# Sparse attention: tile 1's query rotation in quarters after three ticks, and a later place for tile 1's steps

## The chip, the core and the metric

One core of one Trainium2 chip runs the whole program in one launch. The metric is the device time of one execution in microseconds, the median of the runs. A profiled execution lists every instruction of five engines: TensorE (PE, with its weight loads as PEld), VectorE (DVE), ScalarE (ACT), GpSimd (POOL) and SyncE (SP, which issues the DMAs).

## The reference, cut to what matters

Two transformer blocks of two layers each run over 256 tokens of width 1024. The part that the change touches is the attention of the second block's first layer: 16 query heads in 4 groups, three branches (compressed keys, selected blocks, window), weighted by gates. With 256 tokens there are only four blocks of 64 keys, so every block is selected, and the two wide branches are two causal softmaxes.

```python
proj = x @ w_in
q = rope(proj[..., :ATTN_WIDTH].reshape(B, S, N_HEADS_2, hd))
...
s_c = jnp.einsum('bgrqd,bgcd->bgrqc', qb, k_cmp)
p_c = masked_softmax(s_c, cmp_end[None, :] <= t[:, None])
o_c = jnp.einsum('bgrqc,bgcd->bgrqd', p_c.astype(v_cmp.dtype), v_cmp)
...
return gb[:, 0][..., None] * o_c + gb[:, 1][..., None] * o_s + gb[:, 2][..., None] * o_w
```

`rope` multiplies the two halves of each head of 64 by a cosine and a sine table: y1 = x1 c - x2 s and y2 = x2 c + x1 s.

## The kernel before

The 256 tokens are two tiles of 128 (tile 0 and tile 1). Matrix products run as three passes over a high and a low part of each operand (`mm3`, L270 to L274): the high part is a cast on ACT (L264), the low part a subtraction on DVE, or on POOL where `ASIDE` says so (L265; L267 and L268 where a scale comes with it).

Nothing is scheduled at run time: the order of the instructions on each engine is the order in which the program writes them out. Work that is to lie beside other work is a generator. `tick` (L222) advances every waiting generator by one `yield`, and `turnover` (L252) is a tick and a step of the weight stream (`pump`), which splits the next weight blocks into high and low.

In `nsa` (L1322) the query projection of tile 0 runs ahead and that of tile 1 follows block by block (`late`). After a tile's last block `queries(t)` (L1508) is begun as a generator: it rotates the tile's queries out of PSUM with `rope64` (L1306: six DVE instructions, L1314 to L1320, over a number of heads), in two halves of 8 heads with a `yield` after each, and then transposes them in two groups of four (L352) and splits the transposes into `xa` (L267, L268).

The attention of a tile is `unit(t)`: `attend` (L988) runs 16 steps of two heads' scores in a software pipeline. One step of it issues, in this order: s, the scores of step i (L281 and L272 to L274 on PE, into one of two PSUM banks of that tile); e, the exponentials of step i-1 (L1057 on ACT); m, the maxima of step i (L1050 on DVE); c, the weights of step i-2 (L1612, L1614 on DVE, L1073 on POOL); t, the transposes of step i-4 (L1634 on PE, with the high cast L1066); l, their low parts (L1063 on DVE); p, the product with the values of step i-5 on odd steps. Beside it `compressed(t)` computes the scores against the compressed keys (24 products of 32 columns on PE, tile `kc`) and their softmax on DVE (L1562 to L1577), in pieces between ticks.

`weave` (L1003) lays the two tiles' steps in a row by the string `FILL["nsa"]`: "0" and "1" are a step of that tile followed by a tick, "c" is a late block of a projection (nothing where none is left), "w" a block of the output projection. The first "1" begins tile 1's unit, and its `join` finishes `queries(1)` on the spot, whatever it has still to issue:

```python
            def join(t):
                nonlocal wp
...
                self.finish(qs[t])
```

At the first "w" tile 0's remaining steps are issued, at the string's end those of tile 1.

Of the kernel before, what the change touches and what calls it, by code (L numbers as in the profile page):

```python
# [53 lines left out]
POOLED = {"rope": "vv", "nsa": "gg", "fox": "vv"}  # L54
FILL = {"nin": "qlqlqlqlqlqqllqlkklkkkkklkkkkkkkkkllll",
        "da": "c0c0c0c0c0011011100101101010ww1w111w",
        "nsa": "ccc00c0c10c0010010010010111010101001011101w00w0u10",
        "fox": "0cc0cc0c0c0c0111010101011010011w1w1w1w"}
WARM = {"da": (1, 1), "nsa": (0, 0), "fox": (0, 0)}
ASIDE = {"go": "0234567", "wo": "0234567", "w10": "03", "w11": "", "nwo": "034567", "fwo": "0123457"}  # L60
DONE = object()

# [12 lines left out]
class Stream:  # L75
# [11 lines left out]
    def aside(self, key):  # L87

        name, c = key[:-1], key[-1]
        while isinstance(name, tuple):  # L90
            name = "".join(str(x) for x in name) if not isinstance(name[0], tuple) else name[0]
        return str(c) in ASIDE.get(name, "")

# [110 lines left out]
class Build:  # L204
# [883 lines left out]
    def diff_attention(self, xt, vx):  # L1088
# [3 lines left out]
        with tc.tile_pool(name="da", bufs=1) as gp, tc.tile_pool(name="daw", bufs=2) as wp:  # L1092
# [48 lines left out]
            def unit(t):  # L1141
# [68 lines left out]

                return self.attend(H, ORDER["da"], WARM["da"], s=scores, m=peak, e=soft, c=scale, t=turn, l=low, p=pv)

# [109 lines left out]
    def nsa(self):  # L1322
# [3 lines left out]
        with ExitStack() as ctx:  # L1326
# [12 lines left out]
            wq = ctx.enter_context(tc.tile_pool(name="nar", bufs=2))  # L1339
# [168 lines left out]
            def queries(t):  # L1508
                x = self.scr()
                x3 = x.rearrange("p (h d) -> p h d", d=64)  # L1510
                if POOLED["rope"][t] == "g":
                    y = self.scr()
                    for q in range(2):
                        nc.scalar.copy(y[:, HALVES[q]], self.A[t].halves[q])
                        self.rope64(x3[:, 8 * q:8 * q + 8], y[:, HALVES[q]].rearrange("p (h d) -> p h d", d=64), t, 8,
                                    wq, nc.gpsimd)
                        yield
                else:
                    for q in range(2):
                        self.rope64(x3[:, 8 * q:8 * q + 8], self.A[t].halves[q].rearrange("p (h d) -> p h d", d=64), t,  # L1520
                                    8, wq)
                        yield
                for _ in range(WAITS["q"]):
                    yield
                yield from self.transpose_split(x, qT, 0, 8, slice(t * P, t * P + P), 0.125)

            qs, tails = [], []
            steps = {"q": self.ahead([("n0", c) for c in range(KC)], xt, lambda t: qs.append(self.begin(queries(t)))),
                     "k": compress()}
            for i, x in enumerate(FILL["nin"]):  # L1530
# [52 lines left out]
            def unit(t):  # L1583
# [88 lines left out]

                return self.attend(16, ORDER["nsa"], WARM["nsa"], s=scores, m=peak, e=soft, c=scale, t=turn, l=low, p=pv)

# [8 lines left out]
    def fox(self):  # L1683
# [3 lines left out]
        with ExitStack() as ctx:  # L1687
# [108 lines left out]
            def unit(t):  # L1796
# [61 lines left out]

                return self.attend(8, ORDER["fox"], WARM["fox"], s=scores, m=peak, e=soft, c=scale, t=turn, l=low, p=pv)

# [365 lines left out]
```

## Time and profile before

| what | value |
|---|---|
| time, median of 3 runs | 2741.74 us (2736.85 to 2742.47) |
| profiled execution: its own time | 2738.46 us |
| its span, first to last instruction | 2736.4 us |
| PE busy | 2660.6 us (97%) |
| DVE busy | 2033.9 us (74%) |
| ACT busy | 1337.7 us (49%) |
| POOL busy | 142.6 us (5%) |
| mean granted TensorE clock | 0.981 of full |

The page gives busy times over the whole span; a stage is read from the stretches. The attention that the change touches lies from 806 us to 906 us of the span: it begins with tile 0's first scores and ends where the output projection takes PE over. A row of the timeline reads: start, duration (both us), engine, line, operation, written tile, read tiles, shapes, and in brackets the idle time of the engine before it with what ended it. Two instructions that follow each other on one engine overlap a little in their records, so the price of one in a chain is the distance of the starts. PEclk is the granted clock of TensorE: 1.00 is 2.4 GHz and 0.50 is 1.2 GHz.

### The profile page before, as it was taken

The numbers are of one execution on the slowest core, as the hardware profiler recorded it, in microseconds if no ns is written. First come the engines' busy times: TensorE is split into PE (matmuls) and PEld (weight loads), VectorE is DVE, ScalarE is ACT, GpSimd is POOL, SyncE is SP. The second block draws the span as 40 slices with busy tenths as digits, with TensorE's granted clock in tenths as the row PEclk, the third lists the DMA queues.
The fourth block names the chain that finished last, engine by engine and source line by source line (L and its number), as shares of the span: only waits on it lengthen the run. The fifth ranks groups of instructions, "written<-read, shape, count | busy, mean of one in ns | idle before, by whom it ended". The sixth has DMA issues, their size and how long they took to land.

```text
span 2736.4 us, 44261 instructions
## 1 busy us (share of the span) xinstructions
PE 2660.6 (97%) x17478; PEld 2306.4 (84%) x17478; DVE 2033.9 (74%) x3494; ACT 1337.7 (49%) x2061; POOL 142.6 (5%) x130
## 2 busy tenths in 40 slices
PE   8999999999879999999999999999999999999999
PEld 6789777898757899999977788877999999877887
DVE  6655766655776689988899865555799888899654
ACT  5554654545555544444444454454444444444543
POOL 2200021000123000000000000020000000000000
PEclk9999999999988999999999999998999999999999
DMA  6555552563550336655555575451366555555753
GB/s 234 187 195 177 167 162 76 190 190 128 175 192 1 131 111 192 183 177 168 170 169 170 173 235 187 141 168 46 120 190 185 186 167 172 164 171 171 237 190 107
DMA packets 125235, 448.40 MB, mean 164 GB/s; under 512 B 15058, under 2 KB 15586, under 8 KB 125028
## 3 DMA queue, kind: packets, MB, share of 16 engines
q1 hardware_dynamic: 122404, 437.45, 50.3%
q0 software_dynamic: 2624, 8.14, 1.0%
q8 instruction: 136, 2.23, 0.3%
q14 instruction: 71, 0.58, 0.1%
HBM read 444.49 MB, written 1.05 MB: 163 GB/s over the span
## 4 chain that ended last, share of the span: by engine, by line
PE 60%; DVE 6%; ACT 1%; issue 1%; DMA 0%; ACTq 0%
PE A L536 25%; PE B L272 8%; PE B L274 8%; PE B L273 8%; PE A L464 6%; PE B L2046 2%; DVE lob L265 2%; PE B L352 0%; PE A L436 0%; DVE topi L1903 0%; DVE topi L1906 0%; PE A L272 0%; PE B L1835 0%; DVE top L1905 0%; DVE oh L1948 0%
## 5 line engine op out<-in xcount | busy, mean ns | idle before, releaser
L264 ACT CAST hib<-raw 128x1024 fp32r<-128x1024 f32 x519 | 544.3, 1051 | 735.6 <-PE B L274 349.4
L265 DVE TENSOR_TENSOR lob<-raw,hib 128x1024 fp32r<-128x1024 f32 x508 | 619.5, 1221 | 193.8 <-ACT hib L264 193.6
L272 PE MATMUL B<-xa,hib 128*128 128x256 f32 x2096 | 593.1, 283 | 0.0
L273 PE MATMUL B<-xa,lob 128*128 128x256 f32 x2096 | 587.6, 280 | 0.2
L274 PE MATMUL B<-xa,hib 128*128 128x256 f32 x2096 | 586.7, 280 | 0.0
L536 PE MATMUL A<-hib,xa 128*128 128x512 f32 x1440 | 411.7, 399 | 2.0 <-ACT xa L264 2.0
L273 PEld LDWEIGHTS B<-xa,lob 128*128 128x128 f32 x2096 | 394.6, 188 | 1.5 <-DVE lob L265 1.2
L272 PEld LDWEIGHTS B<-xa,hib 128*128 128x128 f32 x2096 | 394.5, 188 | 0.0
L274 PEld LDWEIGHTS B<-xa,hib 128*128 128x128 f32 x2096 | 394.3, 188 | 0.0
L536 PEld LDWEIGHTS A<-hib,xa 128*128 128x128 f32 x1440 | 265.7, 188 | 62.5 <-ACT xa L264 2.4
L265 DVE TENSOR_TENSOR lox<-raw,hix 128x1024 fp32r<-128x1024 f32 x174 | 212.3, 1232 | 120.6 <-ACT hix L264 120.4
L264 ACT CAST hix<-raw 128x1024 fp32r<-128x1024 f32 x192 | 198.2, 1044 | 137.9 <-PE A L536 85.5
L536 PE MATMUL A<-lob,xa 128*128 128x512 f32 x720 | 226.7, 396 | 0.0
L2053 DVE SCALAR_TENSOR_TENSOR H<-B,H 128x512 f32<-128x512 f32 x128 | 170.3, 1332 | 2.3 <-PE B L2046 1.9
L536 PEld LDWEIGHTS A<-lob,xa 128*128 128x128 f32 x720 | 135.2, 188 | 32.8
L464 PE MATMUL A<-hix,xb 128*128 128x512 f32 (+1 forms) x520 | 157.3, 400 | 3.7 <-ACT gates L1423 2.6
L536 PE MATMUL A<-hix,xa 128*128 128x512 f32 x480 | 133.3, 395 | 0.0
L268 DVE SCALAR_TENSOR_TENSOR lox<-raw,gcol,hix 128x1024 fp32r<-128x1024 f32 (+1 forms) x75 | 92.8, 1250 | 36.2 <-ACT hix L267 36.1
L464 PE MATMUL A<-hix,xa 128*128 128x512 f32 x380 | 114.5, 402 | 3.0 <-ACT hix L267 3.0
L464 PEld LDWEIGHTS A<-hix,xb 128*128 128x128 f32 x520 | 95.8, 193 | 24.2 <-ACT gates L1423 3.9
L536 PEld LDWEIGHTS A<-hix,xa 128*128 128x128 f32 x480 | 90.0, 187 | 22.0
L265 DVE TENSOR_TENSOR xa<-H,xa 128x256 fp32r<-128x256 f32 x256 | 106.2, 419 | 2.9 <-ACT xa L264 2.9
(518 smaller groups left out, 4678.2 us busy)
## 6 DMA issues: line engine op xcount, KB each, us to landing
raw<-in_u SPq DMA_DIRECT2D x256, 512.0 KB, 3.6
raw<-in_v SPq DMA_DIRECT2D x256, 512.0 KB, 3.7
raw<-in_f_w_down SPq DMA_DIRECT2D x64, 512.0 KB, 4.5
raw<-in_w_up SPq DMA_DIRECT2D x48, 512.0 KB, 3.7
raw<-in_l_w_in SPq DMA_DIRECT2D x40, 512.0 KB, 3.9
raw<-in_b_w_qkv SPq DMA_DIRECT2D x24, 512.0 KB, 4.2
raw<-in_a_w_in SPq DMA_DIRECT2D x16, 512.0 KB, 5.2
raw<-in_f_w_up SPq DMA_DIRECT2D x16, 512.0 KB, 3.7
```

Source lines behind the costliest of these rows:

```text
L264: nc.scalar.copy(hi, src)
L265: engine.tensor_tensor(lo, src, hi.bitcast(F32), op=ALU.subtract)
L268: nc.vector.scalar_tensor_tensor(lo, src, scale, hi.bitcast(F32), op0=ALU.mult, op1=ALU.subtract)
L272: mm(out, s[0], m[0], start=start, stop=False, **kw)
L273: mm(out, s[1], m[0], start=False, stop=False, **kw)
L274: mm(out, s[0], m[1], start=False, stop=stop, **kw)
L464: self.nc.tensor.matmul(out[:, 512 * q:512 * q + n], xs[u], w[v][:, n * q:n * q + n], start=start and i == 0, stop=stop and i == 2)
L536: self.nc.tensor.matmul(self.A[t][:, n0:n0 + 512], x[u][:, ts_], w[v][:, n0:n0 + 512], start=first and q == 0, stop=last and q == 2)
L2046: nc.tensor.matmul(p[:, t, :], A[:, t].rearrange("p a b -> p (a b)"), B[q][:, t].rearrange("p a b -> p (a b)"), start=q == 0, stop=q == 1)
L2053: nc.vector.scalar_tensor_tensor(hv, p, 1.0 / G_SCALE, hv, op0=ALU.mult, op1=ALU.mult)
```

## The change

`queries` gets a wait in ticks before the rotation, none for tile 0 and three for tile 1. The rotation is done in four quarters of 4 heads instead of two halves of 8; tile 0 still yields after every second quarter, tile 1 after each. The string puts eight "0" ahead of the first "1" instead of three; from there the two strings run alike but for one "1" fewer ahead of the output projection (15 instead of 16).

```diff
-        "nsa": "ccc00c0c10c0010010010010111010101001011101w00w0u10",
+        "nsa": "ccc00c00c0c0c0010010010010111010101001011101w00w0u10",
...
+ROPE_WAIT = (0, 3)
...
-                    for q in range(2):
-                        self.rope64(x3[:, 8 * q:8 * q + 8], self.A[t].halves[q].rearrange("p (h d) -> p h d", d=64), t,
-                                    8, wq)
+                    for _ in range(ROPE_WAIT[t]):
                         yield
+                    for q in range(4):
+                        self.rope64(x3[:, 4 * q:4 * q + 4], self.A[t].halves[q // 2][:, q % 2 * 256:q % 2 * 256 + 256]
+                                    .rearrange("p (h d) -> p h d", d=64), t, 4, wq)
+                        if t or q % 2:
+                            yield
```

What this does to the order is seen at three places. Line numbers of the changed kernel are higher by 1 up to the rotation and by 4 behind it.

First, DVE around tile 1's rotation (written to `scr` from the banks `A_69` and `A_70`). Before, the halves stand ahead of and behind the value splits `vc`, and the first maxima (L1050) come behind both:

```order
L265 TENSOR_TENSOR kc_5618<-B_71,kc_5617 64x4x16 x2
L1314 TENSOR_TENSOR scr_6429<-A_69,rope_tab_5606 128x8x32
L1315 TENSOR_TENSOR rw_6430<-A_69,rope_tab_5606 128x256
L1316 TENSOR_TENSOR scr_6429<-scr_6429,rw_6430 128x8x32
L1317 TENSOR_TENSOR scr_6429<-A_69,rope_tab_5606 128x8x32
L1319 TENSOR_TENSOR rw_6435<-A_69,rope_tab_5606 128x256
L1320 TENSOR_TENSOR scr_6429<-scr_6429,rw_6435 128x8x32
L265 TENSOR_TENSOR vc_5616<-B_72,vc_5615 16x256 x4
L1314 TENSOR_TENSOR scr_6429<-A_70,rope_tab_5606 128x8x32
```

Now the splits and the first two maxima come first, and the first quarter (L1315 to L1321) stands ahead of the first piece of tile 0's compressed softmax (L1566 on) and of the third maxima:

```order
L266 TENSOR_TENSOR vc_5616<-B_72,vc_5615 16x256 x4
L1051 TENSOR_REDUCE sm_6480<-A_67 128x2
L1051 TENSOR_REDUCE sm_6509<-A_68 128x2
L1315 TENSOR_TENSOR scr_6445<-A_69,rope_tab_5606 128x4x32
L1316 TENSOR_TENSOR rw_6511<-A_69,rope_tab_5606 128x128
L1317 TENSOR_TENSOR scr_6445<-scr_6445,rw_6511 128x4x32
L1318 TENSOR_TENSOR scr_6445<-A_69,rope_tab_5606 128x4x32
L1320 TENSOR_TENSOR rw_6516<-A_69,rope_tab_5606 128x128
L1321 TENSOR_TENSOR scr_6445<-scr_6445,rw_6516 128x4x32
L1566 TENSOR_TENSOR scr_6528<-B_73,cmask 128x256
L1568 TENSOR_REDUCE sm_6531<-scr_6528 128x16
L1569 TENSOR_TENSOR scr_6528<-scr_6528,sm_6531 128x256
```

The other three quarters follow one each behind the third, fourth and fifth maxima; twelve DVE instructions of 256 elements have become 24 of 128, for tile 0 as well, whose quarters stand where its halves stood.

Second, PE at tile 0's first scores (bank `A_67`). Before, the first four transposes of tile 1's rotated queries (L352) stand between the scores of step 0 and the compressed scores (`kc`), and the other four behind step 1:

```order
L272 MATMUL A_67<-nkT_5611,xa_84 128x2x128
L273 MATMUL A_67<-nkT_5611,xa_85 128x2x128
L274 MATMUL A_67<-nkT_5612,xa_84 128x2x128
L352 MATMUL B_71<-ident,scr_6429 128x128 x4
L272 MATMUL B_73<-kc_5617,xa_84 128x32
```

Now they stand behind the transposes of steps 1 and 2, ahead of steps 6 and 7; here the first four:

```order
L274 MATMUL A_68<-nkT_5611,xa_85 128x2x128
L275 MATMUL A_68<-nkT_5612,xa_84 128x2x128
L1638 MATMUL B_72<-ident,e_6539 128x128 x2
L353 MATMUL B_71<-ident,scr_6445 128x128 x4
L282 LDWEIGHTS identb
L282 MATMUL A_67<-maskb,identb 128x2x128
```

Tile 1's first scores and its 24 compressed scores, which stood behind step 2 of tile 0, now stand behind step 7.

Third, PE where two steps of tile 1 follow each other with no product between them (a score group into `A_69`, four transposes, a score group into `A_70`). Before, the program has two such pairs; this is the second:

```order
L272 MATMUL A_70<-nkT_5611,xa_84 128x512
L273 MATMUL A_70<-nkT_5611,xa_85 128x512
L274 MATMUL A_70<-nkT_5612,xa_84 128x512
L1634 MATMUL B_72<-ident,e_7112 128x128 x4
L281 LDWEIGHTS identb
L281 MATMUL A_69<-maskb,identb 128x2x128
L272 MATMUL A_69<-nkT_5611,xa_84 128x512
```

Now there are four, two of them in one run of three steps:

```order
L275 MATMUL A_69<-nkT_5612,xa_84 128x512
L1638 MATMUL B_72<-ident,e_6796 128x128 x4
L282 LDWEIGHTS identb
L282 MATMUL A_70<-maskb,identb 128x2x128
L273 MATMUL A_70<-nkT_5611,xa_84 128x512
L274 MATMUL A_70<-nkT_5611,xa_85 128x512
L275 MATMUL A_70<-nkT_5612,xa_84 128x512
L1638 MATMUL B_71<-ident,e_6850 128x128 x4
L282 LDWEIGHTS identb
L282 MATMUL A_69<-maskb,identb 128x2x128
```

The other two stand further on, close to the end of tile 1's scores. SP's DMAs stand in the same order in both programs.

## Rows read from the trace of the kernel before

**Rows 1.** The page: the granted clock in 40 slices of the span, in tenths.
```profile
PEclk9999999999988999999999999998999999999999
```

**Rows 2.** Stretches: start:end length, busy PE PEld DVE ACT POOL, PEclk, DMA, GB/s.
```profile
806.00:820.00 14.00, 9.95 (x43) 8.69 (x43) 11.58 (x19) 5.42 (x12) 5.58 (x5) 0.50 0.45 161
820.00:838.75 18.75, 17.79 (x64) 13.31 (x64) 10.90 (x38) 6.07 (x29) 3.32 (x6) 0.50 0.00 0
887.00:890.00 3.00, 3.00 (x16) 3.00 (x15) 1.13 (x4) 1.73 (x6) 1.04 (x1) 0.50 0.00 0
```

**Rows 3.** PE's waits, 745 to 905 us: total, times, longest.
```profile
PE B L352 <- DVE scr L1320: 7.9, 3, 3.9
```

**Rows 4.** Timeline: a rotation of keys (4 heads), tile 0's first half, PE behind it.
```profile
744.88 0.28 DVE L1314 TENSOR_TENSOR dup<-k,rope_tab 128x128 f32<-128x128 f32 x1
...
746.34 0.28 DVE L1314 TENSOR_TENSOR dup<-k,rope_tab 128x128 f32<-128x128 f32 x1
...
754.61 0.41 DVE L1314 TENSOR_TENSOR scr<-A,rope_tab 128x256 f32<-128x256 f32 x1
...
756.50 0.43 DVE L1320 TENSOR_TENSOR scr<-scr,rw 128x256 f32<-128x256 f32 x1
...
756.99 1.07 PE L352 MATMUL B<-ident,scr 128*128 128x128 f32 x4 [3.88 <-DVE scr L1320]
```

**Rows 5.** Timeline: tile 1's second half beside POOL's splits, and PE behind it.
```profile
809.08 0.42 DVE L265 TENSOR_TENSOR vc<-B,vc 16x256 fp32r<-16x256 f32 x1 [0.43 <-ACT vc L264]
...
811.05 2.38 POOL L265 TENSOR_TENSOR lox<-raw,hix 128x1024 fp32r<-128x1024 f32 x1 [4.97 <-ACT hix L264]
...
813.96 2.36 POOL L265 TENSOR_TENSOR lox<-raw,hix 128x1024 fp32r<-128x1024 f32 x1
...
814.41 2.20 DVE L1320 TENSOR_TENSOR scr<-scr,rw 128x256 f32<-128x256 f32 x1
...
816.66 1.12 PE L352 MATMUL B<-ident,scr 128*128 128x128 f32 x4 [3.82 <-DVE scr L1320]
```

**Rows 6.** A stretch that holds tile 0's compressed softmax on DVE.
```profile
819.50:823.55 4.05, 4.05 (x14) 2.67 (x13) 3.72 (x14) 1.81 (x9) 0.61 (x1) 0.50 0.02 9
```

**Rows 7.** Timeline: exponentials of one step on ACT, first and last row.
```profile
817.03 0.37 ACT L1057 ACTIVATE e<-A,sm 128x128 f32<-128x128 f32 x1 [4.50 <-issue]
...
817.63 0.20 ACT L1057 ACTIVATION_READ_ACCUMULATOR e<-A,sm 128x1 f32 x1
```

**Rows 8.** Timeline: PE, pieces at the low and at the full clock.
```profile
805.94 0.42 PE L281 MATMUL A<-maskb,identb 128*128 128x256 bf16 x1
...
822.52 0.39 PE L272 MATMUL B<-kc,xa 128*128 128x32 f32 x1
...
825.74 0.40 PE L281 MATMUL A<-maskb,identb 128*128 128x256 bf16 x1
...
827.01 0.39 PE L272 MATMUL B<-kc,xa 128*128 128x32 f32 x1
...
831.86 0.37 PE L281 MATMUL A<-maskb,identb 128*128 128x256 bf16 x1 [0.96 <-ACT e L1057]
...
833.10 0.69 PE L1634 MATMUL B<-ident,e 128*128 128x128 f32 x2
...
837.54 0.56 PE L272 MATMUL B<-pt,nv 128*128 128x256 f32 x1
...
838.97 0.30 PE L281 MATMUL A<-maskb,identb 128*128 128x256 bf16 x1
...
841.13 0.27 PE L281 MATMUL A<-maskb,identb 128*128 128x256 bf16 x1
...
841.88 0.44 PE L1634 MATMUL B<-ident,e 128*128 128x128 f32 x2
```

**Rows 9.** Timeline: PE at the two pairs of tile 1's steps.
```profile
855.87 0.27 PE L281 MATMUL A<-maskb,identb 128*128 128x256 bf16 x1 [1.11 <-ACT e L1057]
...
885.60 0.27 PE L281 MATMUL A<-maskb,identb 128*128 128x256 bf16 x1 [1.16 <-ACT e L1057]
```

## The prediction

> **What bounds the kernel now.** First the granted clock on the page: full in nearly every slice, with its two lowest slices around 800 us [rows 1]. Then the stretches there: from 806 to 838.75 us, the head of the attention that the change reorders, PE runs at half clock; in the first 14 us of it it is busy for 9.95, in the 18.75 behind them for 17.79 [rows 2]. Then who is waited for: of PE's waits between 745 and 905 us the largest in total is for `scr` of L1320, the last instruction of a query rotation, 7.9 us in three waits [rows 3]. The timeline gives two of them: 3.9 us for tile 0's first half at 757 us [rows 4] and 3.8 us for tile 1's second half at 816.7 us [rows 5]; the third is what is left, 0.2. So PE bounds this stage, and it loses time by two waits for a rotation on DVE and by the low clock. The edit to tile 1 aims at the second wait; the first is tile 0's and is only made longer.
>
> **Tile 0's rotation in four pieces.** Six DVE instructions over 8 heads take 2.32 us (from 754.61 to the end of L1320 at 756.93); six over 4 heads take 1.46 (744.88 to 746.34) [rows 4]. A half as two quarters is 2.92, so 0.60 more, twice. PE sits idle ahead of 757 us until the first half is done [rows 4], so the first 0.60 has no cover. The second stands behind it on DVE ahead of the split that PE's next transposes need. I take both, **+1.2 us**; the low end is 0, if the weight loads behind it set the pace until 800 us anyway, and the high end 1.3.
>
> [...]
>
> **Tile 1's rotation moved: the wait that goes.** Gone are the 3.8 us and the 0.2 behind the halves. What is late next has to be followed through DVE, in its new order: value splits, maxima 0 and 1, quarter 1, first piece of the compressed softmax, maxima 2, quarter 2, second piece, maxima 3, quarter 3, maxima 4, quarter 4, maxima 5. PE's order is scores 0, 15 compressed products, scores 1, 9 of them, scores 2, scores 3 and so on; scores 3 use the bank of scores 1 and wait for exponentials 1, and on ACT these stand behind the exponential of the compressed softmax.
>
> PE at half clock: a score group is 1.27 us (825.74 to 827.01), 15 compressed products 3.22 (822.52 to 825.74), so 9 are 1.93 [rows 8]. From 805.94, where the scores of step 0 start [rows 8], scores 2 end at 805.9 + 3 x 1.27 + 5.15 = 814.9. On DVE the four splits `vc` stand 0.85 apart (0.42 of work, 0.43 of wait for ACT); the third started at 809.08 with the first half's last instructions ahead of the first, and without these I take the fourth to end near 809.5 instead of 810.4 [rows 5]; maxima 0 behind them, maxima 1 once scores 1 end (811.7). Quarter 1 starts at 812.1 and comes to its last instruction at 813.4. That one, like L1320 of before, reads two tiles of SBUF, and the rows show what that costs beside POOL: 2.20 us, from 814.41 to 816.61, while POOL's split ran from 813.96 to 816.32; alone it was 0.43 [rows 4, 5]. POOL's two splits come some 0.9 us earlier than before, since ACT casts for them right behind `vc`: the second runs from 813.1 to 815.5. So quarter 1 ends at 815.7.
>
> [...]
>
> From 815.7 the first piece of the softmax takes 1.3 (three instructions [rows 6]), its exponential on ACT 0.4, exponentials 1 0.8 (817.03 to 817.83) [rows 7]: scores 3 start at 818.3. PE idles from 814.9 to 818.3, **3.4 us in place of 4.0**. The wait has changed its name, not gone.
>
> **Then DVE sets the pace.** From 815.7: piece one 1.3; second piece 2.1 (the stretch of 4.05 us holds both pieces, one maxima and two small operations [rows 6]); three quarters 3 x 1.46; four maxima 4 x 0.45; three pairs of small operations and a fourth 4 x 0.35; two low parts 2 x 0.42; the split of PE's new transposes 0.7. Sum 12.5, to 828.2. PE has less than that to do there (scores 3 to 6, four transposes twice) and idles for it in two more pieces. Behind 828.2 follow two transposes, six products, four transposes, scores 7 and two transposes. A pair of transposes is recorded with 0.69, which overlaps the next instruction by some 0.2, so 0.5; the six products are 1.43 (837.54 to 838.97) [rows 8]; four transposes are recorded with 1.12 [rows 5], and I take 0.7. That is 0.5 + 1.43 + 0.7 + 1.27 + 0.5 = 4.4: PE stands at 832.6 with steps 0 to 7 of tile 0 scored. At 839.0 in the trace, where the distances between PE's instructions turn to those of the full clock, steps 0 to 6 were scored and, of tile 1, two steps and the 24 compressed products. What the new program has more to do from there: 24 compressed products, 5.15 at half clock and 3.0 at full by the ratio of the score groups (0.75 to 1.27 [rows 8]); two score groups of tile 1, taken as 1.1 each at full clock (1.5 x 0.75, twice the columns in three of four products); less one score group and two transposes of tile 0, 1.05. That is 4.2, so 836.8 against 839.0: **-2.2 us**, if the clock is full from 832.6 on. Before, it rose at 839.0, 7.1 us after PE's last idle time ended at 831.86 [rows 8]; from 828.2 the same gives 835.4, 2.8 us at half clock, which costs 1.2. **Front of the attention: -1.0.** If the clock rises only behind tile 1's compressed products, near 842.6, the cost is 4.1 and the front ends at +1.9. In the trace it did not rise while PE went through 24 of them from 822.52 on [rows 2, 8], so I give this a large share.
>
> **The later steps.** At both pairs of tile 1's steps with no product between, PE waited 1.1 and 1.2 us for exponentials [rows 9]. The new order has four such pairs: two more, **+2.2**; from 0 (other waits fall in the same place) to 5.3, where each also drops the clock as the second did: 3 us of busy PE at half clock behind it, 1.5 lost [rows 2]. One step of tile 1 more stands behind the two blocks of the output projection; its chain to the transposes has 5 us of PE's products over it, and I take 0. SP's order is unchanged, and no transfer moves.
>
> **Sum.** 1.2 - 1.0 + 2.2 = +2.4 us. Against the profiled execution's own 2738.46 that is 2740.9; that execution lies 3.3 below the median, and the same 2.4 on the median of 2741.74 gives **2744.1**.
>
> **The rivals.**
>
> Slower: the clock. If it stays low until tile 1's compressed products are through (front +1.9) and falls at each added pair (2.2 + 3.0), the sum is 1.2 + 1.9 + 5.2 = +8.3, 2750.0. It decides between 832 and 836 us: a clock that has not risen when those products begin. For it: they are 5 us of narrow products, and they now stand in the dense part. Against it: one of the two pairs of before (855.9) left the clock alone.
>
> Faster: with the long wait cut up, the clock comes back during steps 3 to 7 and not at 839. Then PE's pieces behind 828.2 run at full speed (2.6 instead of 4.4, by the ratio of the score groups), the front is 828.2 + 2.6 + 4.2 - 839.0 = -4.0, and with ACT and DVE ahead by then the pairs of tile 1 wait for nothing, which gives back 1.1, 1.2 and the 1.5 behind it: 1.2 - 4.0 - 3.9 = -6.7, 2735.0. For it: no single wait is as long as the 3.8 us that went. Against it: PE still idles three times ahead of 828.
>
> No effect: the rotation is as long as the stage's slack, tile 0's 1.2 vanish in the waits for weights, and the pairs' waits move elsewhere: 2741.7. That the change doesn't do what it says is excluded by its order.
>
> **How the numbers follow.** About 0.2% (5.5 us) is what a measurement of this kernel can tell from no change. Forecast 0.42, slower 0.24, faster 0.20, no effect 0.14. Forecast and no effect lie within 0.2%: same 0.56, faster 0.20, slower 0.24. The range takes in both rivals' times but for their outer halves: 2735 to 2751. The forecast's own, by the bounds of its terms, is 2739 to 2750.
>
> **What would show it.** Right: a DVE rotation instruction of 2 us or more beside a split of POOL near 813 to 816, PE's wait there now for exponentials and no longer for `scr` of L1320, of about 3.4 us; tile 0's first wait near 4.5 us; clock low from 798 to at least 832; four waits of about 1.1 us at tile 1's pairs. Wrong: a full clock ahead of 828, no wait over 2 us between 812 and 820, or a stage from 806 us to the output projection that is shorter or longer than its 100 us by over 6.

## The result and the profile after

The changed kernel takes 2759.12 us, the median of seven runs (2751.50 to 2765.13), against 2740.44 (2736.85 to 2742.47) before on the same chip: the ratio is 1.0064, with a 95% interval of 1.0055 to 1.0074. It is slower by some 19 us, outside the predicted range, which ended at 2751. Its profiled execution took 2755.32 us with a span of 2753.1, 16.7 more than before's, at a mean granted clock of 0.976 (before 0.981).

The page of the changed kernel, the granted clock in 40 slices, beside [rows 1]:

```profile
PEclk9999999999976999999999999998999999999999
```

Only the two slices of 757 to 895 us differ in the clock, 7 and 6 where 8 and 8 stood. The stretches there (start:end, length, PE's busy time, clock, DMA share, GB/s), beside [rows 2]:

```profile
806.00:820.00 14.00, 8.44 (x48) 0.64 0.59 196
809.33:809.83 0.50, 0.50 (x4) 0.99 1.16 475
809.83:810.33 0.50, 0.50 (x3) 0.50 0.74 262
...
830.00:861.00 31.00, 30.61 (x114) 0.50 0.00 1
861.00:868.00 7.00, 5.87 (x31) 0.99 0.00 0
868.00:874.70 6.70, 5.54 (x20) 0.50 0.00 0
874.70:922.00 47.30, 41.08 (x265) 1.00 0.00 1
```

The row from 830 to 861 us is the one to look at. PE has next to no idle time left, and it works 31 us at a granted clock of 0.50, the low clock; before, the clock was full from 839 us on, but for 3.4 us at 887. Behind the first added pair of tile 1's steps it falls once more. The two short rows show where the long low stretch begins, at 809.8 us; before it began at 798.0. So it does not only end later, it also begins later (with 3.4 us of low clock from 799.6 on ahead of it). Where the text ahead of the prediction and some expectations speak of 2.4 and 1.2 GHz, the traces show a pace: a product of 512 columns (bf16) takes 0.43 us at 0.50 (ten 4.45 in e3, nine 4.02 in e4) and 0.216 at 1.00 (twelve 2.76 in e11, four 1.03 in e5), which is 1.2 and 2.4 columns a nanosecond. PE's waits in the stage (timeline of the changed kernel; in brackets the idle time ahead and who ended it), beside [rows 5] and [rows 9]:

```profile
812.51 0.37 PE L282 MATMUL A<-maskb,identb 128*128 128x256 bf16 x1 [0.73 <-ACT e L1058]
818.65 0.37 PE L282 MATMUL A<-maskb,identb 128*128 128x256 bf16 x1 [4.83 <-ACT e L1058]
823.11 0.37 PE L282 MATMUL A<-maskb,identb 128*128 128x256 bf16 x1 [1.27 <-ACT e L1058]
830.44 1.12 PE L353 MATMUL B<-ident,scr 128*128 128x128 f32 x4 [0.39 <-DVE cT L266]
...
866.99 0.27 PE L282 MATMUL A<-maskb,identb 128*128 128x256 bf16 x1 [1.11 <-ACT e L1058]
870.51 0.37 PE L282 MATMUL A<-maskb,identb 128*128 128x256 bf16 x1 [1.16 <-ACT e L1058]
...
888.26 0.41 PE L1638 MATMUL B<-ident,e 128*128 128x128 f32 x2 [1.06 <-DVE pt L1064]
...
895.90 0.27 PE L282 MATMUL A<-maskb,identb 128*128 128x256 bf16 x1 [1.16 <-ACT e L1058]
902.56 0.27 PE L282 MATMUL A<-maskb,identb 128*128 128x256 bf16 x1 [1.16 <-ACT e L1058]
911.96 0.39 PE L273 MATMUL B<-pt,nv 128*128 128x256 f32 x1 [0.85 <-ACT pt L1067]
...
915.98 0.36 PE L273 MATMUL B<-pt,nv 128*128 128x256 f32 x1 [0.61 <-DVE sm L1616]
```

**An account of the stage.** It is taken from the transposes of L1483 (792.6 us before, 795.3 after) to the start of the last product with the values. Three things are read from each trace: the length, the sum of PE's waits in brackets, and PE's busy time at the low clock. If busy time at the low clock costs double, then the length less the waits less half of that busy time is the work at full clock, which must be the same in every kernel with the same instructions on PE. It is, within 1.4 us:

| kernel | length | waits | busy at the low clock | half of it | what is left |
|---|---|---|---|---|---|
| before | 113.6 | 11.0 | 39.4 | 19.7 | 82.9 |
| after | 126.3 | 17.4 | 52.9 | 26.5 | 82.4 |
| after, second profile (e12) | 123.7 | 18.4 | 44.9 | 22.5 | 82.8 |
| order of the steps alone (e1) | 124.7 | 21.5 | 41.5 | 20.8 | 82.5 |
| quarters and wait alone (e2) | 117.0 | 16.7 | 32.9 | 16.5 | 83.8 |
| weight splits moved (e6) | 123.6 | 17.1 | 47.0 | 23.5 | 83.0 |
| stall added to before (e8) | 119.2 | 18.5 | 35.2 | 17.6 | 83.1 |

So in the profiled execution the stage is 12.7 us longer, 6.4 by waits and 6.8 by the clock. The two are not independent: where the clock falls later, PE reaches its next wait earlier and waits longer there. In e8, whose front is that of before, it fell at 807.8 us in place of 798.0, and the wait at 808 us was 3.63 us in place of 0.23. Of the other 4.0 us of the span, 1.6 were there before 703 us, where the programs are alike, 1.1 come up to 796 us (tile 0's rotation), and 1.3 lie behind the stage.

**The same over many runs.** Each run gives its span and mean granted clock, and 2 x (1 - clock) x time is the time at the low clock, if that is 0.50 everywhere, as it is in the low stretches shown here. Runs of one and the same kernel differ in it: 94 runs of the kernel before, taken beside the experiments, have clocks of 0.975 to 0.984 and times of 2756.3 to 2734.0 us, in two groups: 71 up to 2743.6 us and 23 from 2747.1 on. Within kernels the time grows by 0.39 us for each microsecond at the low clock (a fit over all runs with a level for each kernel). With that slope the difference from before's mean (2742.6) splits into a part by the clock and a rest:

| kernel | ratio to before, 95% interval | median | mean against before | us at the low clock (before 109) | by the clock | rest |
|---|---|---|---|---|---|---|
| after (ratio and median of 7 runs; the rest with e12's 6) | 1.0064 [1.0055, 1.0074] | 2759.1 | +15.9 | 135 | +10.3 | +5.7 |
| e1: order alone | 1.0042 [1.0022, 1.0063] | 2750.9 | +11.7 | 122 | +5.3 | +6.5 |
| e2: quarters and wait alone | 1.0018 [1.0003, 1.0033] | 2745.0 | +3.4 | 110 | +0.6 | +2.8 |
| e6: after, splits moved | 1.0042 [1.0025, 1.0058] | 2751.3 | +10.8 | 124 | +6.1 | +4.7 |
| e8: before, stall added | 1.0023 [1.0003, 1.0042] | 2745.3 | +5.6 | 113 | +1.7 | +3.9 |
| e3: after, products at 811 | 1.0063 [1.0033, 1.0092] | 2755.2 | +17.2 | 137 | +11.2 | +6.0 |
| e5: after, products at 845 and in pairs | 1.0027 [1.0007, 1.0047] | 2750.4 | +6.7 | 107 | -0.6 | +7.2 |
| e9: after, products at 833 to 847 and in pairs | 1.0028 [1.0009, 1.0046] | 2749.8 | +8.3 | 110 | +0.5 | +7.8 |
| e10: after, products in pairs | 1.0037 [1.0016, 1.0058] | 2751.7 | +9.3 | 124 | +6.1 | +3.2 |
| e4: before, products at 811 | 0.9995 [0.9975, 1.0016] | 2737.6 | -2.0 | 103 | -2.1 | +0.2 |
| e7: before, products at three places | 0.9968 [0.9951, 0.9985] | 2735.4 | -8.5 | 82 | -10.5 | +2.0 |
| e11: e7 and twelve more | 0.9993 [0.9977, 1.0010] | 2736.8 | -3.4 | 88 | -8.1 | +4.7 |

Two of e10's twelve runs took 3694.9 and 5849.7 us, and its row leaves them out. The rest of the changed kernel, 5.7, is somewhat under what its trace shows of waits, 6.4 in the stage and 1.1 ahead of it. The clock's part is 10.3 by the runs and 6.8 in the profiled pair. So the clock is half of the loss (of the stage, in the profiled pair) to two thirds (of the whole, over the runs), and the other part is waits.

Half of the low time is the price for the part in which PE is busy (half of 52.9 us closes the changed kernel's account); over whole runs a microsecond at the low clock costs 0.39. That PE also waits at the low clock explains a part of this: in that stage 61.4 us are low and 52.9 of them busy, which makes 0.43 of the low time.

### The profile page after: what moved, and what is told of

It is laid out like the page before. It is cut to its first block, busy times and chain, and to the rows that moved or that the text cites. A ratio compares the mean times of both kernels' runs of the same rounds, so it can differ in the third digit from the quotient of the medians.

```text
span 2753.1 us, 44292 instructions
## 1 busy us (share of the span) xinstructions
PE 2670.5 (97%) x17478; PEld 2311.4 (84%) x17478; DVE 2035.3 (74%) x3518; ACT 1336.9 (49%) x2061; POOL 142.3 (5%) x130
## 4 chain that ended last, share of the span: by engine, by line
PE 59%; DVE 6%; ACT 1%; issue 1%; DMA 0%; ACTq 0%; DVEq 0%
PE A L537 25%; PE B L273 8%; PE B L275 8%; PE B L274 8%; PE A L465 6%; PE B L2050 2%; DVE lob L266 2%; PE A L437 0%; PE B L353 0%; PE B L1839 0%; DVE topi L1907 0%; DVE topi L1910 0%; DVE top L1909 0%; DVE oh L1952 0%; DVE wk L1908 0%
```

## The experiments

The clock theory: the new order leaves PE at the low clock much longer, and that is most of the loss. The theory of the waits: the added waits, and the quarters beside GpSimd's splits, are the loss themselves.

### One part of the change at a time: e1 and e2

```diff
# e1 (against before): the order alone
-        "nsa": "ccc00c0c10c0010010010010111010101001011101w00w0u10",
+        "nsa": "ccc00c00c0c0c0010010010010111010101001011101w00w0u10",
# e2 (against before): everything else
+ROPE_WAIT = (0, 3)
...
-                    for q in range(2):
...
+                    for _ in range(ROPE_WAIT[t]):
                         yield
+                    for q in range(4):
...
```

> The kernel before with the changed order of tile 1's steps alone: rotations in halves, no wait of three ticks. Clock theory (most of the 14.8 us of the stage from tile 0's first scores to the projection is TensorE work done at 1.2 GHz between 833 and 861 us): the order alone starves TensorE in the first steps, so the clock stays at 0.50 well past 839 us and the time is +8 to +16 us against before. Theory of the waits (the quarters beside GpSimd's split and the 4.83-us wait for exponentials that came with them): without the quarters the time is within +4 us of before.

> The change's quarters and its wait of three ticks, with the old order of tile 1's steps. Clock theory: tile 1's step 0 waits for a rotation that now begins later, so TensorE's wait ahead of it grows from 3.8 us to 5 to 8 us, the clock comes back within 10 us behind it, and the time is +1 (tile 0's rotation in quarters) to +6 us. Theory of the waits: what the quarters bring is nearly all of it, +10 to +17 us.

e1 is +10.4 us by the median, where the clock theory had +8 to +16 and the theory of the waits at most +4: the order is most of the loss, and it doesn't need the quarters. Stretches of e1 (PE's busy time, clock):

```profile
834.50:838.00 3.50, 3.50 (x24) 0.99 0.00 0
...
841.30:844.80 3.50, 3.25 (x21) 0.99 0.00 0
844.80:858.40 13.60, 12.96 (x47) 0.50 0.01 2
```

The clock came back twice, for some 3.5 us each, and stayed away until 858 us. But the clock theory had this as the whole, and it is half (5.3 of 11.7 by the table): by the groups of PE's waits from 745 to 925 us (total, times, longest) e1 waits 8.8 us in eight pieces for exponentials, where before it was 3.5 in four:

```profile
PE A L281 <- ACT e L1057: 8.8, 8, 1.4
```

e2 is +4.5 by the median, as the clock theory had it. Its waits are those of a rotation that begins too late for the old place of tile 1's step 0, beside [rows 5]:

```profile
812.96 0.69 PE L353 MATMUL B<-ident,scr 128*128 128x128 f32 x2 [2.40 <-DVE scr L1321]
816.53 0.69 PE L353 MATMUL B<-ident,scr 128*128 128x128 f32 x2 [2.88 <-DVE scr L1321]
820.01 0.69 PE L353 MATMUL B<-ident,scr 128*128 128x128 f32 x2 [2.78 <-DVE scr L1321]
```

What it said of the clock was wrong: it came back at 849.3 us, 29 us behind the last of these waits and not within 10. Neither part gains anything by itself.

### Dense products in the first waits: e3 and e4

Products of an identity that nobody reads (bf16, 128x512) are put into PE's queue at the end of a step; the same lines serve all the kernels below:

```diff
+HOT = ({2: 10}, {})     # e3, against after: per tile {step: products}
+HOT = ({1: 9}, {})      # e4, against before
...
             for k, f, b in order:
...
+            self.warm(hot.get(i, 0))
             yield
...
```

> The changed kernel with ten products of 128x512 added, whose result nobody reads, behind the scores of tile 0's step 2, where TensorE waits 4.83 us for exponentials. Clock theory: the granted clock rises to 1.00 by 825 us in place of 861 us, the stage loses 12 to 19 us, and the time is 2738 to 2747 us. Theory of the waits: the clock may rise, but the stage stays at least 10 us longer than before's 100.4 us, and the time is 2752 to 2762 us.

> The kernel before with nine such products behind the scores of tile 0's step 1, where TensorE waits 3.82 us for tile 1's rotation. Clock theory: the clock rises to 1.00 by 822 us in place of 839 us; TensorE's work of 819 to 839 us goes at up to twice the speed, 6 to 10 us less where nothing else takes over, so 2731 to 2735 us. Theory of the waits: those of the exponentials and of the gathers take the place, and the time is within 3 us of before.

Stretches of e3, then of e4:

```profile
816.00:819.40 3.40, 1.72 (x9) 0.99 0.01 5
819.40:840.00 20.60, 19.41 (x75) 0.50 0.00 0
...
843.30:877.50 34.20, 31.63 (x108) 0.50 0.00 0
```

```profile
816.00:819.30 3.30, 3.30 (x24) 1.00 0.56 205
819.30:826.00 6.70, 6.70 (x30) 0.50 0.00 0
```

In both, the products filled the wait and the clock rose right behind them, at 816 us. In both it fell again within 3.5 us. In e3 PE had waited 2.36 us for the next exponentials; in e4 it had not waited at all. The changed kernel with them is no faster (2755.2, as the theory of the waits had it), and the clock theory's 2738 to 2747 fell: in neither trace did one burst bring the clock back for good. e4 is 2737.6, within the 3 us that the theory of the waits allowed; its interval contains no change.

### The rival: GpSimd's splits and a stall by itself: e6 and e8

```diff
# e6, against after: two weight splits on VectorE
-ASIDE = {..., "nwo": "034567", ...}
+ASIDE = {..., "nwo": "0345", ...}
# e8, against before: six fills on VectorE behind tile 0's step 5
+STALL = ({5: 6}, {})
...
+            if i in hot:
+                idle = self.scr()
+                for _ in range(hot[i]):
+                    self.nc.vector.memset(idle, 0.0)
```

> The changed kernel with two of the weight splits (chunks 6 and 7) on VectorE in place of GpSimd, so that no rotation instruction runs beside one on GpSimd (1.87 and 2.49 us there, 0.28 to 0.56 us elsewhere). Theory of the waits: the 4.83-us wait for exponentials shrinks to 1 to 3 us, and with it the time, by 2 us or more against the changed kernel (2757 us or less). Clock theory: the wait may shrink, but the low clock lasts to 850 us or longer all the same, and the time stays within 4 us of the changed kernel.

> The kernel before with six fills of a 128x1024 tile added on VectorE behind tile 0's step 5, at some 829 us, 3 to 6 us that delay the maxima ahead of the next exponentials, so that TensorE waits there 3 to 6 us once more. Theory of the waits: the kernel grows by that wait alone, +3 to +6 us. Clock theory: the wait also starts the time at 1.2 GHz anew, which then lasts to 846 us or longer in place of 839 us: +6 to +14 us, more than the wait itself.

e6: the rotation's last instruction is short again, and the stall is still there, its long wait in two pieces (timeline, DVE and PE):

```profile
808.43 0.37 PE L282 MATMUL A<-maskb,identb 128*128 128x256 bf16 x1 [2.54 <-ACT e L1058]
...
810.11 0.29 DVE L1321 TENSOR_TENSOR scr<-scr,rw 128x128 f32<-128x128 f32 x1
...
812.85 0.37 PE L282 MATMUL A<-maskb,identb 128*128 128x256 bf16 x1 [3.11 <-ACT e L1058]
...
817.30 0.37 PE L282 MATMUL A<-maskb,identb 128*128 128x256 bf16 x1 [1.26 <-ACT e L1058]
```

2.54, 3.11 and 1.26 are 6.91 us, where the changed kernel has 0.73, 4.83 and 1.27, 6.83 in all. Beside the splits these two instructions had cost VectorE 3.8 us more (1.87 and 2.49 in place of 0.29 each); now there stand the two splits of 1.22 us and a wait of 0.64 for their casts. So the stall is no shorter, and the run can't say what it would be without that cost and without the splits. The median fell by 7.8 us all the same. The theory of the waits had "2 us or more", but its reason did not hold: of the 5.1 us between the means 4.2 are the clock, and its trace has 47.0 us of busy low clock in place of 52.9. The clock theory's "within 4 us" did not hold either; its clock was low to 851 us, with 3.4 us of full clock from 837.7 on. As a test of what that cost is worth over the whole kernel it stays inconclusive.

e8: the six fills ran from 836.5 to 843.4 us, later than I had taken, and PE waited 3.81 us at the next transposes. PE's row behind the fills, and the stretches:

```profile
845.00 0.66 PE L1639 MATMUL B<-ident,e 128*128 128x128 f32 x2 [3.81 <-DVE cT L266]
```

```profile
845.00:852.00 7.00, 7.00 (x25) 0.50 0.00 0
852.00:860.00 8.00, 7.68 (x43) 0.99 0.01 3
```

+5.6 by the mean, 3.9 of it the rest, about the wait itself: the forecast of the waits theory held. But the run doesn't refute the other one, whose "low to 846 us or longer" came too: the low stretch lasted to 852.2. It had begun at 807.8 where before's began at 798.0, and so the low time of the stage is 44.4 us in both. The clock was back 7.2 us behind the wait, as it was 7.1 behind the last one of before [rows 8]. That is the distance on which my prediction counted.

### Dense products where PE is busy at the low clock, and in the pairs: e5, e9, e10, e12

```diff
+HOT = ({}, {1: 8, 4: 4, 5: 4, 11: 4, 13: 4})                       # e5, against after
+HOT = ({7: 2, 8: 3, 9: 3}, {0: 4, 4: 4, 5: 4, 11: 4, 13: 4})       # e9, against after
+HOT = ({}, {4: 4, 5: 4, 11: 4, 13: 4})                             # e10, against after
# e12: the changed kernel itself, once more
```

> The changed kernel with products of 128x512 that nobody reads at five places behind tile 1's steps: eight behind step 1 (848 us in its trace, TensorE busy without a gap at 1.2 GHz), four each behind steps 4, 5, 11 and 13, in the waits of 1.1 us for exponentials. Clock theory, with the addition that what the steps of 835 to 861 us give TensorE lies near the edge of what brings the clock back: the clock rises by 853 us in place of 861 us and doesn't fall again at 868 us; at most 3.4 us of added work, 4 us saved ahead of 861 and 3.4 us behind it: 4 us less than the changed kernel to the same (2753 to 2759 us). Theory of the waits: the products change nothing but their own time, 0 to 3.4 us more than the changed kernel.

> The changed kernel with products of 128x512 that nobody reads in the stretch in which its clock stayed at 0.50 though TensorE was busy (833 to 847 us: four behind tile 1's step 0, two, three and three behind tile 0's steps 7, 8 and 9), and four each in the four waits of 1.1 us of tile 1's pairs. Clock theory: the clock is back by 845 us in place of 861 and the dip at 868 us is gone, so 8 + 3.4 us saved for at most 5 us of added work: 2746 to 2753 us, 6 to 12 us less than the changed kernel. Theory of the waits: added work only, the same as the changed kernel or up to 5 us more.

> The changed kernel with four products of 128x512 that nobody reads in each of the four waits of tile 1's pairs alone. Clock theory: the dip at 868 us (6.8 us at 0.50) is gone and the stretch ahead of 861 us stays as it was: 2 to 4 us less than the changed kernel. Theory of the waits (the pairs cost their 1.1 us each, and nothing behind them): no change, within 1.5 us.

> The changed kernel once more, beside the three above on the same chip, to see whether its long stretch at 1.2 GHz returns. Clock theory: it does, within 10 us of 861 us where it ends, and the time is 2754 to 2763 us. If the stretch were an accident of the one profiled run, it would end near 840 us and the time would be near 2745 us.

Stretches of e12 (with one row of PE's timeline), e5, e9 and e10, in this order:

```profile
842.00:845.00 3.00, 2.26 (x12) 0.90 0.00 0
845.14 0.37 PE L282 MATMUL A<-maskb,identb 128*128 128x256 bf16 x1 [0.89 <-ACT e L1058]
845.00:858.00 13.00, 12.86 (x47) 0.50 0.00 1
866.00:872.00 6.00, 4.84 (x20) 0.52 0.00 0
```

```profile
842.00:845.00 3.00, 3.00 (x18) 1.00 0.00 0
845.00:858.00 13.00, 12.76 (x75) 1.00 0.00 1
866.00:872.00 6.00, 5.97 (x38) 1.00 0.00 1
```

```profile
842.00:845.00 3.00, 3.00 (x19) 1.00 0.00 0
866.00:872.00 6.00, 5.97 (x39) 1.00 0.02 4
```

```profile
845.00:858.00 13.00, 13.00 (x45) 0.50 0.00 0
866.00:872.00 6.00, 5.70 (x34) 0.98 0.00 0
```

e12: 2759.5 us, ratio 1.0065 [1.0041, 1.0088], as the clock theory had it. The long low stretch returned, until 858 us, with 3.4 us of full clock in between (841.0 to 844.4), and so did the dip behind the pair.

The pairs: with four products in each wait the dip behind 867 us is gone in e5 and e9, and in e10 the clock, once back at 866.2, stays. The waits themselves shrank, here in e10 beside 1.16 of the changed kernel:

```profile
892.13 0.27 PE L283 MATMUL A<-maskb,identb 128*128 128x256 bf16 x1 [0.30 <-ACT e L1060]
```

e10 is some 7 to 8 us under the changed kernel by the medians (2 to 4 were expected by the clock theory, none by the other); its trace shows the dip gone and nothing more that its products would explain: the long low stretch lasted to 866.2.

The long stretch: e9 was forecast at 2746 to 2753 us and took 2749.8; its clock was back at 841.6. But e5 and e12 speak against the reading that its products brought the clock back. In e5 the clock was back at 841.9 us, and its first added products ran from 844.7 us on; in e12, which has none, it was back at 841.0. Up to there both have the instructions of the changed kernel, whose first profile had 861.0; e10 has them too, and its clock was back at 828.6 us, for 3.4 us. So the order makes a long low stretch more likely (over the runs 135 us at the low clock, before 109) but doesn't fix it.

What the products may do is hold the clock. In e12 PE came to a wait of 0.89 us for exponentials at 844.3 us, and from 844.4 on the clock was low for 13.7 us; in e1 it fell at the same wait (0.89 us, clock low from 844.8 on). In e5 eight products filled this place, and the clock stayed. That is one profile of each, so it is likely and not shown; and a wait is not the only way to lose the clock, since in e4 it fell without one.

e5 took 2750.4 us, under the range of either theory (the lower one began at 2753): against the changed kernel its clock's part is 10.9 lower and the rest 1.5 higher. And what the products in e9 win by the clock, they cost in PE's time: against e10, whose pairs are filled alike, the clock's part is 5.6 lower and the rest 4.6 higher.

### A version that beats both: e7 and e11

```diff
+HOT = ({1: 9, 4: 3, 5: 3}, {0: 4, 5: 4, 13: 4})           # e7, against before
+HOT = ({0: 12, 1: 9, 4: 3, 5: 3}, {0: 4, 5: 4, 13: 4})    # e11, against before
```

> The kernel before with the nine products of 128x512 that nobody reads in its 3.82-us wait, and more of them: three each behind tile 0's steps 4 and 5, four behind tile 1's step 0 (the stretch 819 to 836 us that stayed at 0.50 with the nine alone), four each in the two later waits of 1.1 us. Clock theory: the low stretch behind 819 us shrinks from 17 to 10 us or less and the dips at 853 and 884 us go; 3.5 us + 3.4 us gained less up to 3.4 us of added work: 2731 to 2736 us. Theory of the waits: added work only, 2738 to 2743 us.

> The kernel before with all that the last one had (nine products in the wait for the second half of tile 1's rotation, ten among the compressed products, eight in the pairs' waits) and twelve more behind tile 0's step 0, in the wait of 3.2 us for the first half. Clock theory: the low stretch of 802 to 812 us shortens to 7 us or less, of which 1 to 2 us count, since VectorE sets the pace there: 2731 to 2736 us. Theory of the waits: 2736 to 2742 us.

Stretches of e7 that answer to those of e4 above and to [rows 2]:

```profile
819.30:826.00 6.70, 6.70 (x24) 0.50 0.00 0
826.00:836.00 10.00, 9.77 (x56) 1.00 0.01 2
```

The clock is back at 826 us, where it was 836 with e4's nine products alone and 839 before, and neither of the pairs' waits has a dip behind it. e7 takes 2735.4 us, as the clock theory had it, ratio 0.9968 [0.9951, 0.9985]: faster than the kernel before, by clock alone (-10.5, for 2.0 of added work and waits). Twelve products more in the wait ahead of it (e11) gave nothing further: 2736.8, as the theory of the waits had it, and its interval contains no change. PE waits there for VectorE's rotation (3.23 us in e7, and in e11 still 0.70 behind the twelve products), so the low clock seems to have been free at that place.

## Why the prediction was wrong, point by point

**Tile 0's rotation, +1.2: right.** The wait of [rows 4] became two (below), and the programs, 1.6 us apart at 703 us, were 2.9 apart at 769 and 2.7 at 796. Five more traces with the quarters (e2, e3, e6, e10, e12) lose 1.3 us from 703 to 769 us, and e1, without them, loses nothing there:

```profile
757.80 0.44 PE L353 MATMUL B<-ident,scr 128*128 128x128 f32 x2 [3.11 <-DVE scr L1321]
759.25 0.69 PE L353 MATMUL B<-ident,scr 128*128 128x128 f32 x2 [1.01 <-DVE scr L1321]
```

**The wait that changes its name: mechanism right, size short.** POOL's splits and quarter 1, beside [rows 5]:

```profile
810.76 2.38 POOL L266 TENSOR_TENSOR lox<-raw,hix 128x1024 fp32r<-128x1024 f32 x1 [1.89 <-ACT hix L265]
...
811.41 1.87 DVE L1317 TENSOR_TENSOR scr<-scr,rw 128x128 f32<-128x128 f32 x1
...
813.65 2.41 POOL L266 TENSOR_TENSOR lox<-raw,hix 128x1024 fp32r<-128x1024 f32 x1
...
813.72 2.49 DVE L1321 TENSOR_TENSOR scr<-scr,rw 128x128 f32<-128x128 f32 x1
```

Not one but both instructions of quarter 1 that read two SBUF tiles fell into splits, 1.87 and 2.49 us. The trace of before shows the same of its second half, beside the 2.20 of L1320:

```profile
811.17 2.54 DVE L1316 TENSOR_TENSOR scr<-scr,rw 128x256 f32<-128x256 f32 x1
```

The wait for exponentials was 4.83 and not 3.4. Only 0.35 of the difference is a later end, scores 3 at 818.65; the other 1.1 is an earlier start, scores 2 done at 813.8 in place of 814.9, since the clock was full up to 809.8. That clock was a miss of its own: I had it low from 798 on. Around the long wait stand 0.73, for exponentials 0, which my path had left out, 1.27 and 0.39: 7.2 us of waits in the front, where 5.3 were before (0.2, 3.8, 0.96 and 0.3). The term was -0.6 and is +1.9. In e6, where no split on POOL runs beside them, both instructions take 0.29 us.

**VectorE sets the pace until PE stands at 832.6: right, the number partly by luck.** Tile 0's step 7 was scored and its transposes done at 833.1. But the stage had begun 2.7 us later than before; from its first transposes it is 37.8 us in place of the 40.0 of the forecast, and PE's full clock up to 809.8, which I had not counted on, came ahead of it.

**The clock, at 835.4 or near 842.6 at the latest: the step that failed.** I took the 7.1 us between PE's last wait and the rise, read once in the trace of before, for the clock's distance from any last wait, and put the cost of the low clock behind it at 1.2 us, or 4.1 at most. In the changed kernel the last wait ended at 830.44 and the clock came back at 861.0, 30.6 us later, with PE busy in 30.61 of 31 us. In other traces that distance is 7.2 us (e8), 11.9 (e12, from 829.1), 12.8 (e5, from 829.2) and 16 (e2, from 833.2), and in e10 it is 1.1, from 827.5. The rival "slower: the clock" had the two places right, tile 1's compressed products and the added pairs, and the price too low: it ended the low stretch with those products, near 842.6 (they ended near 844), and the stretch lasted 17 us longer.

**The pairs, +2.2: right.** Four waits of 1.11 to 1.16 us where two of 1.1 and 1.2 were [rows 9], +2.3. One dip of the clock went with them, at the first two.

**"One step of tile 1 more ... I take 0": wrong, +2.2.** Besides the pairs, PE waits 3.9 us from 886 us to the last product, for the parts of transposed weights (`pt`) and once for VectorE's sums ahead of them (`sm`; 1.06, 0.85 and 0.61 are the longest), where before it waited 1.65 (0.28, 0.53, 0.30, 0.32, 0.22). e1 has the same waits and e2 has not, so it is the order. The products that I had put over the last step's chain are there: its transposes, at 918.1, come without a wait, and behind them PE waits 0.33 and 0.23, where before it was 0.32 and 0.22. What came on top stands ahead of it: 1.06 at tile 0's last pair of transposes, and 0.85 and 0.23 behind eight transposes of tile 1 at 909.7, with only three products between the transposes and the wait.

Together: my waits came to +1.6 (-0.6 and 2.2) and were +6.4; my clock came to -0.4 and was 6.8 in the profiled pair, 10.3 over the runs. Of my signs of being wrong two came: the clock was full ahead of 828 us, up to 809.8, and the stage from the first scores on, which was to stay within 6 us of its 100, took 115.

**What stays open.** What in the stretch from 830 to 861 us keeps the clock low. The compressed products run in the middle of it, from 835 to 844 us, but behind them PE does what it did in before while the clock rose, and stays at 0.50 for 17 us more. Equal instructions first had it back at 828.6 in one run, 841.0 and 841.9 in two and 861.0 in a fourth. No run took the compressed products out.

## What to carry to other kernels

TensorE's clock was half or more of what this order cost (6.8 of 12.7 us in the stage, 10.3 of 15.9 over the runs), so an order is to be priced with the clock that it leaves: price a stage as its work at full clock, plus its waits, plus half of the busy time at the low clock, and check that the first term stays the same from kernel to kernel (here 82.4 to 83.8 us). A distance read once between a wait and the clock's return is no constant (7.1 us before, from 1.1 to 30.6 in the six other traces named above), so give the end of a low stretch a range as long as the stage. When two interleaved streams are shifted against each other, look at the end as well as at the front: there the later one has less of the other's work beside it, and waits come into the open (3.9 us from 886 us on, before 1.65).

## What the runs showed of the hardware that was not expected

TensorE can work with next to no gap and stay at a granted clock of 0.50: 30.61 of 31 us in the changed kernel, 12.86 and 13.00 of 13 in e12 and e10. One program gives low stretches of different lengths from run to run (the changed kernel's ended at 861.0 us in one profile and at 841.0, then 858, in the other), and the scatter goes with them: over 94 runs of the kernel before the clock goes from 0.975 to 0.984 and the time from 2756.3 to 2734.0 us. And work that nobody needs can pay: the 27 products of e7 take off 5.4 us by the medians.
